# One 64-column product in place of two 32-column products in a hybrid attention and DeltaNet layer

## The chip, the core and the metric

The kernel runs on one core of a Trainium2 chip. The metric is the device time of one execution in microseconds (us), lower is better. Four compute engines with separate instruction streams share the core's memory: TensorE (PE: matmuls into PSUM, with PEld for its weight loads), VectorE (DVE), ScalarE (ACT) and GpSimd (POOL). SyncE (SP) issues the transfers. PSUM has eight banks of 128 partitions by 512 fp32 values here, and the kernel hands them out itself.

## What is computed

One layer over 512 latent tokens and 256 context tokens, width 1024: a modulated RMS norm, one input projection, two mixers side by side (windowed attention, and a gated DeltaNet in both directions), a gated merge, an output projection and an MLP of width 4096. The change lies in the DeltaNet, in its chunked form with chunks of 64 tokens and 8 heads of 64:

```python
def gated_delta_chunked(q, k, v, g_log, beta, s0):
    ...
    kk = jnp.einsum('bhnid,bhnjd->bhnij', kc, kc)
    t_mat = jnp.eye(CHUNK, dtype=jnp.float32) + bc[..., :, None] * dec_strict * kk
    ...
    w_mat = lax.linalg.triangular_solve(t_mat, (bc * eG)[..., None] * kc, ...)
    u_v = lax.linalg.triangular_solve(t_mat, bc[..., None] * vc, ...)
    intra = dec_incl * jnp.einsum('bhnid,bhnjd->bhnij', qc, kc)
    ...
```

`kk` (keys against keys) and `intra` (queries against keys) are 64 by 64 matrices, one for each chunk and head: 4 context and 8 latent chunks, 8 heads.

## The kernel before

**Half products.** `half_products` (L743 to L755) makes the 64 by 64 matrix of 16 pairs of chunk and head pair at a time (a group: four chunks, four head pairs `q`; the two heads of a pair are the two halves `a` of the partitions). Each matrix is cut into four 32 by 32 blocks. For a half `h` of the chunk's keys as weights (64 partitions by 32 columns), x = 0 multiplies with the same half of the chunk (a block on the diagonal, into bank `D_`), x = 1 with the other half (a block off the diagonal, into bank `O_`). So a pair has 8 calls of `PE.matmul` at L754 (two x, two `h`, two `a`), a group 128. All are fp32, and the hardware makes two weight loads and two matmuls of each call. Output partitions are `quad(a, h)`: the four combinations of `a` and `h` use four different tiles of the array. After 8 of the 16 pairs the generator yields, and its caller lets other work in.

**Where it is called.** `chunk_mats(gi)` (L757 to L798) runs for `gi` = 0 (context), 1 and 2 (latent) with keys on both sides. It takes the banks `kD` and `kO`, makes the products, then for each of two directions multiplies masks with the decay (L768, L772), sums the decays by two matmuls each into `dp` and `dO` (L773, L774), takes Exp on ACT (`act`, whose line is L148), and multiplies by beta and mask (L784) and by `kD` (L786). Last it does the same for the off-diagonal part (L793, L794 with `kO`), and frees the banks. This runs woven with the attention's input projections (`in_tile_steps`, matmuls at L313 to L315 of `mm3`; QK norm with L439 on PE, L442 to L450 on DVE, L436 and L437 on ACT). The matrices then go to `invert_all`: a forward substitution on DVE (L827, L828), woven in the same manner.

The second call stands in the main body (L1225 to L1236, called IA stage here): for g = 0 and 1 the queries are multiplied with the keys of group 1 + g, into banks `qD` and `qO`; DVE multiplies by the decay (L1233 for each direction, L1234) and ACT spreads the result (L1241 to L1243). Between the halves PE gets matmuls of the gate tiles as fill (`run_fill`, L998). Behind it come the steps of the scan (`chain_step`, L1110 to L1159), whose first lines do not need these results.

**What sets the order.** Program order and the weaving are written by hand; a scheduler at build time then moves independent instructions of an engine against each other as operands and banks come free. Each engine runs its stream in order. `bank(n)` takes n neighbouring free banks in rotation; in the IA stage four of the eight are held by `zb` (L1093). Input-projection weights go through a cast on ACT (L259) and a subtraction on DVE (L262) before PE can use them (L315 needs L262's result).

Of the kernel before, what the change touches and what calls it, by code (L numbers as in the profile page):

```python
# [12 lines left out]
ALU = mybir.AluOpType  # L13
# [31 lines left out]
CH = 64  # L45
HC = CH // 2
# [53 lines left out]
def tile_layer(ctx: ExitStack, tc: tile.TileContext, I: dict, out: bass.AP, dbg=None):  # L100
    nc = tc.nc
    V, A, G, PE = nc.vector, nc.scalar, nc.gpsimd, nc.tensor
# [19 lines left out]
    alloc, bank = mem.get, lambda n=1: banks.get(n * 512)  # L122
# [17 lines left out]
    def act(out_, in_, func, **kw):  # L140

        sets = TABLES.get(func)
        if sets and actg["set"] not in sets:
            head = A.preload_act_table_set(sets[0])
            for o in actg["ops"]:
                tc.add_manual_dep(head.ins, o.name, nosync, reason="table sets")
            actg.update(set=sets[0], head=head.ins, ops=[head.ins])
        r = A.activation(out_, in_, func, **kw)  # L148
        if sets:
            tc.add_manual_dep(r.ins, actg["head"].name, nosync, reason="table sets")  # L150
            actg["ops"].append(r.ins)
        return r
# [183 lines left out]
    for kt in range(KT):  # L336
        t = alloc(512)
        o = kt * 1024
        hx.append(modulate(t.ap, xt[kt], rx, modA[:, kt, 0:1], modS[:, kt, 0:1],
                           H[:, o:o + 512], H[:, o + 512:o + 1024]))  # L340
        h = alloc(512)
# [313 lines left out]
    kT = [alloc(TOK, True) for _ in range(4)]  # L655
# [37 lines left out]
    def col(c):  # L693

        return SEQ + c * CH if c < NCC else (c - NCC) * CH
# [3 lines left out]
    quad = lambda a, h: slice(64 * a + 32 * h, 64 * a + 32 * h + 32)  # L699
# [38 lines left out]
    ED = [alloc(1024, True) for _ in range(2)]  # L738
    EO = alloc(1024, True)
    NTO = [alloc(512, True) for _ in range(3)]  # L740
    v3 = lambda ap, n=HC: ap.rearrange("p (m i) -> p m i", i=n)

    def half_products(D_, O_, gi, src):  # L743

        for i in range(16):
            if i == 8:
                yield
            c, q = gi * 4 + i // 4, i % 4
            for x, dst in enumerate((D_, O_)):
                for h in range(2):  # L750
                    for a in range(2):
                        r = slice(64 * a, 64 * a + 64)
                        o, o2 = col(c) + HC * h, col(c) + HC * (h ^ x)
                        PE.matmul(dst[quad(a, h), i * HC:(i + 1) * HC], kT[q][r, o:o + HC], src[q][r, o2:o2 + HC],  # L754
                                  start=True, stop=True)  # L755

    def chunk_mats(gi):  # L757
        ms = slice(gi * 16, gi * 16 + 16)
        kD, kO = bank(), bank()
        for _ in half_products(kD, kO, gi, kT):  # L760
            for _ in range(HPAUSE):
                yield
        yield
        dO = bank()
        for d in range(2):
            mg, mb = alloc(1024), alloc(512)
            row = lambda m_: m_[:, d, :].unsqueeze(1).broadcast_to([P, 16, HC])
            V.tensor_tensor(v3(mb.ap), row(nmask), bc(btok[:, d, ms], HC), op=ALU.mult)  # L768
            dp = bank()
            for x in range(2):  # L770
                gx = mg[:, x * 512:x * 512 + 512]
                V.tensor_tensor(v3(r32(gx)), row(mi), bc(gsp[:, x, d, ms], HC), op=ALU.mult)  # L772
                PE.matmul(dp.ap, trr[:, d, :], r32(gx), start=(x == 0), stop=(x == 1))  # L773
                PE.matmul(dO.ap, trr[:, 2 + d, :], r32(gx), start=(d == x == 0), stop=(d == x == 1))  # L774
            mg.free()
            if gi == 0:
                eb = alloc(512)
                e, na = eb.ap, neg[0][:, d * 512:d * 512 + 512]
            else:
                o = (gi - 1) * 512  # L780
                e, na = ED[d][:, o:o + 512], neg[1 + d][:, o:o + 512]
            act(e, dp.ap, AF.Exp)
            dp.free()
            V.tensor_tensor(e, e, mb.ap, op=ALU.mult)  # L784
            mb.free()
            V.tensor_tensor(na, e, kD.ap, op=ALU.mult)  # L786
            if gi == 0:
                eb.free()
            yield
        eb = alloc(512) if gi == 0 else None  # L790
        e = eb.ap if gi == 0 else EO[:, (gi - 1) * 512:gi * 512]
        act(e, dO.ap, AF.Exp)
        V.tensor_tensor(v3(e), v3(e), bc(tbO[:, ms], HC), op=ALU.mult)  # L793
        V.tensor_tensor(NTO[gi].ap, e, kO.ap, op=ALU.mult)  # L794
        for b in (kD, kO, dO, eb):
            if b:
                b.free()
        yield  # L798
# [92 lines left out]
    qT = []  # L891
# [8 lines left out]
    def mats():  # L900
        for q in range(4):
            l2n(kT[q].ap, 1.0, ((0, SEQ), (SEQ, TOK)), epsc, False)
            yield
        for gi in range(3):
            yield from chunk_mats(gi)
# [179 lines left out]
    def run_fill(n):  # L1085
        for _ in range(n):
            next(fill, None)
# [126 lines left out]
    for g in range(2):  # L1214
        ms = slice(16 * g, 16 * g + 16)
        f, b = xa[0][:, ms], xa[1][:, ms]
# [7 lines left out]
    ia = [v64(b.ap) for b in IA]  # L1224
    for g in range(2):  # L1225
        ms = slice(16 * g, 16 * g + 16)
        es = slice(512 * g, 512 * g + 512)
        run_fill(FILL[2] - FPAUSE)
        qD, qO = bank(), bank()
        for _ in half_products(qD, qO, 1 + g, qT):  # L1230
            run_fill(FPAUSE)
        for d in range(2):
            V.tensor_tensor(ia[d][:, ms, :HC], v3(ED[d][:, es]), v3(qD.ap), op=ALU.mult)  # L1233
        V.tensor_tensor(EO[:, es], EO[:, es], qO.ap, op=ALU.mult)  # L1234
        qD.free()
        qO.free()  # L1236
        eo = v3(EO[:, es])
        for a in range(2):
            lo, hi = quad(a, 0), quad(a, 1)
            for d in range(2):  # L1240
                A.activation(ia[d][hi, ms, HC:], ia[d][hi, ms, :HC], AF.Copy)  # L1241
            A.activation(ia[0][lo, ms, HC:], eo[lo], AF.Copy)
            A.activation(ia[1][hi, ms, :HC], eo[hi], AF.Copy)  # L1243
            G.memset(ia[0][hi, ms, :HC], 0.0)
            G.memset(ia[1][lo, ms, HC:], 0.0)
# [52 lines left out]
    for ct in range(8):  # L1298
# [3 lines left out]
        g = gdt[ct].ap  # L1302
# [41 lines left out]
    ms = [(r32(HM[:, k * 1024:k * 1024 + 512]), r32(HM[:, k * 1024 + 512:k * 1024 + 1024])) for k in range(KT)]  # L1344
# [51 lines left out]
    for hf in range(4):  # L1396
        act_ = []
        for f in range(FT):
            if first:
                bufs, _, acc = first.pop(0)  # L1400
# [5 lines left out]
            r, hl = alloc(1024), alloc(1024)  # L1406
# [135 lines left out]
```

## Time and profile before

| | |
|---|---|
| median of 3 runs | 935.47 us (935.13 to 935.96) |
| the profiled execution's own time | 939.21 us |
| its span, first to last instruction | 937.3 us |
| mean granted TensorE clock | 0.991 |
| PE, PEld, DVE, ACT busy, share of the span | 96%, 78%, 64%, 48% |
| PE matmuls, and as many weight loads | 7722 |
| of these at L754 | 1280 |

Terms of the profile: a row "a <- b: us" says that a sat idle until b ended. "Issue" is idle time in which an engine waited for nothing that the profile shows. Rows in order of time have the start, the length and the number of instructions of a run, and in brackets the idle time before it. A matmul's length runs from its start to its modelled end, so the pace of a run of n matmuls is (length of the run minus length of one) / (n - 1).

### The profile page before, as it was taken

How to read it: one execution, taken by the hardware profiler on the slowest of the kernel's cores; microseconds unless marked ns; L12 is line 12 of the kernel's file. 1: busy time of each engine (PE TensorE's matmuls, PEld its weight loads, DVE VectorE, ACT ScalarE, POOL GpSimd, SP SyncE). 2: the span in 40 equal slices, each digit the busy share in tenths (PEclk: the TensorE clock that was granted, in tenths of full speed). 3: DMA queues.
4: the chain of work that ended last, by engine and by line, in shares of the span. 5: the costliest groups of instructions: out<-in, count | busy, mean ns of one | idle time of the engine just before them, and what ended most of it. 6: DMA issues, size and time to landing. Idle time of an engine off the chain costs nothing.

```text
span 937.3 us, 18134 instructions
## 1 busy us (share of the span) xinstructions
PE 902.6 (96%) x7722; PEld 727.8 (78%) x7722; DVE 598.7 (64%) x1021; ACT 448.3 (48%) x827; POOL 12.1 (1%) x26
## 2 busy tenths in 40 slices
PE   8999889989999999989999998999999999999998
PEld 5668667867777677778878888988888888888886
DVE  3588789997887898257865977982455235434411
ACT  5577544347567887475555434560243125213400
POOL 0000000000000002000000000000000000000000
PEclk9999989999999999999999999999999999999999
DMA  9650112110000132225424574481344124222111
GB/s 360 236 198 1 48 47 68 46 45 24 23 13 23 52 108 82 90 93 175 152 83 135 160 267 135 143 288 41 114 146 144 45 68 154 93 68 90 45 43 47
DMA packets 28448, 98.32 MB, mean 105 GB/s; under 512 B 3536, under 2 KB 4176, under 8 KB 27344
## 3 DMA queue, kind: packets, MB, share of 16 engines
q1 hardware_dynamic: 28368, 97.18, 31.7%
q8 instruction: 60, 0.98, 0.4%
q14 instruction: 20, 0.16, 0.1%
HBM read 95.07 MB, written 2.10 MB: 104 GB/s over the span
## 4 chain that ended last, share of the span: by engine, by line
PE 76%; DVE 10%; ACT 6%; DMA 4%; issue 3%; SPq 0%; DVEq 0%; ACTq 0%
PE banks L313 16%; PE banks L314 15%; PE banks L315 15%; PE banks L998 10%; PE banks L1043 2%; PE banks L1110 2%; DMA wr<-in_wm 2%; PE banks L571 1%; DVE wl L262 1%; PE banks L1141 1%; DMA wa<-in_wada 1%; PE banks L1122 1%; DVE m L185 1%; PE banks L577 1%; DVE m L828 1%
## 5 line engine op out<-in xcount | busy, mean ns | idle before, releaser
L313 PE MATMUL banks<-m,m 128*128 128x512 f32 (+1 forms) x600 | 223.6, 378 | 2.7 <-DVE m L620 1.9
L314 PE MATMUL banks<-m,m 128*128 128x512 f32 (+1 forms) x600 | 224.6, 376 | 0.1
L315 PE MATMUL banks<-m,m 128*128 128x512 f32 (+1 forms) x600 | 224.5, 376 | 0.0
L259 ACT ACTIVATE m<-wr 128x1024 fp32r<-128x1024 f32 x68 | 72.1, 1060 | 158.7 <-PE banks L314 79.9
L313 PEld LDWEIGHTS banks<-m,m 128*128 128x128 f32 x600 | 111.9, 188 | 25.5 <-ACT m L319 2.5
L314 PEld LDWEIGHTS banks<-m,m 128*128 128x128 f32 x600 | 112.5, 188 | 22.5 <-issue 1.1
L315 PEld LDWEIGHTS banks<-m,m 128*128 128x128 f32 x600 | 112.5, 188 | 21.6 <-issue 1.2
L262 DVE TENSOR_TENSOR m<-wr,m 128x1024 fp32r<-128x1024 f32 x68 | 83.1, 1224 | 71.2 <-ACT m L259 35.0
L313 PE MATMUL banks<-m,wh 128*128 128x512 f32 (+1 forms) x280 | 104.0, 372 | 0.8 <-ACT wh L259 0.8
L998 PE MATMUL banks<-m,wh 128*128 128x512 f32 x320 | 104.0, 400 | 0.0
L315 PE MATMUL banks<-m,wl 128*128 128x512 f32 (+1 forms) x280 | 101.9, 366 | 1.8 <-DVE wl L262 1.8
L314 PE MATMUL banks<-m,wh 128*128 128x512 f32 (+1 forms) x280 | 101.1, 361 | 0.0
L1426 DVE SCALAR_TENSOR_TENSOR m<-banks,modT,m 128x512 f32<-128x512 f32 x32 | 24.0, 750 | 101.0 <-PE banks L315 101.0
L262 DVE TENSOR_TENSOR wl<-wr,wh 128x1024 fp32r<-128x1024 f32 (+1 forms) x58 | 62.2, 1072 | 28.8 <-ACT wh L259 28.7
L259 ACT ACTIVATE wh<-wr 128x1024 fp32r<-128x1024 f32 (+1 forms) x58 | 54.6, 941 | 30.6 <-PE banks L314 16.8
L998 PEld LDWEIGHTS banks<-m,wh 128*128 128x128 f32 x320 | 59.1, 188 | 12.1
L998 PE MATMUL banks<-m,wl 128*128 128x512 f32 x160 | 64.9, 406 | 0.0
L315 PEld LDWEIGHTS banks<-m,wl 128*128 128x128 f32 x280 | 53.6, 193 | 10.2 <-DVE wl L262 2.6
L313 PEld LDWEIGHTS banks<-m,wh 128*128 128x128 f32 x280 | 54.1, 193 | 9.2 <-ACT wh L259 1.4
L314 PEld LDWEIGHTS banks<-m,wh 128*128 128x128 f32 x280 | 54.1, 193 | 6.9 <-issue 0.2
L184 ACT ACTIVATE m<-m 128x512 fp32r<-128x512 f32 (+1 forms) x56 | 35.2, 631 | 49.2 <-DVE m L1409 21.2
L185 DVE TENSOR_TENSOR m<-m,m 128x512 fp32r<-128x512 f32 (+1 forms) x56 | 38.3, 688 | 18.8 <-ACT m L184 18.3
(236 smaller groups left out, 1298.9 us busy)
## 6 DMA issues: line engine op xcount, KB each, us to landing
wr<-in_wm SPq DMA_DIRECT2D x64, 512.0 KB, 3.5
wr<-in_win SPq DMA_DIRECT2D x38, 512.0 KB, 3.5
wa<-in_wada SPq DMA_DIRECT2D x32, 512.0 KB, 4.3
m<-in_wada SPq DMA_DIRECT2D x8, 1024.0 KB, 11.4
m<-in_xT SPq DMA_DIRECT2D x8, 512.0 KB, 5.3
wr<-in_wbr SPq DMA_DIRECT2D x16, 256.0 KB, 2.6
wr<-in_wout SPq DMA_DIRECT2D x8, 512.0 KB, 4.3
out<-m SPq DMA_DIRECT2D x8, 256.0 KB, 2.0
```

The source lines that it names most:

```text
L184: A.activation(r32(hi), src, AF.Copy)
L185: (eng or V).tensor_tensor(r32(lo), src, hi, op=ALU.subtract)
L259: h = A.activation(r32(hi), raw, AF.Copy)
L262: V.tensor_tensor(r32(lo), raw, hi, op=ALU.subtract)
L313: PE.matmul(acc, w[0][:, k, :], xhi, start=(start and i == 0), stop=False)
L314: PE.matmul(acc, w[0][:, k, :], xlo, start=False, stop=False)
L315: PE.matmul(acc, w[1][:, k, :], xhi, start=False, stop=(stop and i == n - 1))
L571: PE.transpose(pt[:, j * P:(j + 1) * P], probs[j][:, i * P:(i + 1) * P], ident)
L998: PE.matmul(acc.ap, w[x][:, k, :], hx[k][y], start=(k == p == 0), stop=(k == KT - 1 and p == 2))
L1043: PE.matmul(pa.ap, w[x][:, j, :], r32(Q[y][:, :, j, :]), start=(j == p == 0), stop=(j == 3 and p == 2))
L1110: PE.matmul(z[r, x * 256 + q * HD:x * 256 + (q + 1) * HD], src[q][r, col(c):col(c) + CH], S[r, q * HD:(q + 1) * HD], start=True, stop=True)
L1426: V.scalar_tensor_tensor(xn_[ct], acc.ap, modT[:, 3, ct:ct + 1], xn_[ct], op0=ALU.mult, op1=ALU.add)
```

## The change

The two products with x = 0 and x = 1, which have the same weights, become one: the right-hand side is the whole chunk of 64 columns, with its halves in order for `h` = 0 and swapped for `h` = 1, so that the diagonal block comes first in both. A pair of chunk and head pair then takes 4 calls with 64 columns, a group 64 calls, and its output is 64 columns wide, diagonal and off-diagonal block side by side. Eight pairs fill a bank and the group two neighbouring banks, taken by one `bank(2)`. Every reader takes its half as a view: 16 runs of 32 columns, 64 columns apart, over both banks.

```diff
-    def half_products(D_, O_, gi, src):
+    def half_products(dst, gi, src):
...
             c, q = gi * 4 + i // 4, i % 4
-            for x, dst in enumerate((D_, O_)):
-                for h in range(2):
-                    for a in range(2):
-                        r = slice(64 * a, 64 * a + 64)
-                        o, o2 = col(c) + HC * h, col(c) + HC * (h ^ x)
-                        PE.matmul(dst[quad(a, h), i * HC:(i + 1) * HC], kT[q][r, o:o + HC], src[q][r, o2:o2 + HC],
-                                  start=True, stop=True)
+            for h in range(2):
+                for a in range(2):
+                    r = slice(64 * a, 64 * a + 64)
+                    o = col(c) + HC * h
+                    both = src[q][r, col(c):col(c) + CH].rearrange("p (x j) -> p x j", x=2)
+                    PE.matmul(dst[quad(a, h), i * CH:(i + 1) * CH].rearrange("p (x j) -> p x j", x=2),
+                              kT[q][r, o:o + HC], both[:, ::-1] if h else both, start=True, stop=True)
+
+    def diag_off(dst):
+
+        v = dst.ap.rearrange("p (m x i) -> p x m i", x=2, i=HC)
+        return v[:, 0], v[:, 1]
...
-        kD, kO = bank(), bank()
-        for _ in half_products(kD, kO, gi, kT):
+        kk = bank(2)
+        kD, kO = diag_off(kk)
+        for _ in half_products(kk, gi, kT):
...
-            V.tensor_tensor(na, e, kD.ap, op=ALU.mult)
+            V.tensor_tensor(v3(na), v3(e), kD, op=ALU.mult)
...
-        V.tensor_tensor(NTO[gi].ap, e, kO.ap, op=ALU.mult)
-        for b in (kD, kO, dO, eb):
+        V.tensor_tensor(v3(NTO[gi].ap), v3(e), kO, op=ALU.mult)
+        for b in (kk, dO, eb):
...
-        qD, qO = bank(), bank()
-        for _ in half_products(qD, qO, 1 + g, qT):
+        qq_ = bank(2)
+        qD, qO = diag_off(qq_)
+        for _ in half_products(qq_, 1 + g, qT):
             run_fill(FPAUSE)
         for d in range(2):
-            V.tensor_tensor(ia[d][:, ms, :HC], v3(ED[d][:, es]), v3(qD.ap), op=ALU.mult)
-        V.tensor_tensor(EO[:, es], EO[:, es], qO.ap, op=ALU.mult)
-        qD.free()
-        qO.free()
+            V.tensor_tensor(ia[d][:, ms, :HC], v3(ED[d][:, es]), qD, op=ALU.mult)
+        V.tensor_tensor(v3(EO[:, es]), v3(EO[:, es]), qO, op=ALU.mult)
+        qq_.free()
```

The scheduler then places the products and their neighbours anew. In the changed program the products' matmul is still at L754; lines behind it are six higher (L773 is L779, L774 is L780, L998 is L1004, L1110 is L1116).

Two places of PE's stream show it. The first is the second group (`gi` = 1) among the input projections; `m_555` to `m_558` are the keys `kT`, `wh` and `wl` weights of the projection. Before:

```order
L313 MATMUL banks<-m_167,wh_946 128x512
L314 MATMUL banks<-m_167,wh_946 128x512
L754 MATMUL banks<-m_555 32x32 x4
L754 MATMUL banks<-m_556 32x32 x4
...
L439 MATMUL banks<-m_1132,c_bones 128x512
L315 MATMUL banks<-m_167,wl_947 128x512
L754 MATMUL banks<-m_555 32x32 x8
...
L754 MATMUL banks<-m_558 32x32 x8
L313 MATMUL banks<-m_167,wh_946 128x512
```

The same place in the changed program:

```order
L313 MATMUL banks<-m_167,wh_914 128x512
L439 MATMUL banks<-m_1036,c_bones 128x512
L314 MATMUL banks<-m_167,wh_914 128x512
...
L754 MATMUL banks<-m_555 32x64 x4
L754 MATMUL banks<-m_556 32x64 x4
...
L754 MATMUL banks<-m_558 32x64 x4
L315 MATMUL banks<-m_167,wl_915 128x512
L779 MATMUL banks<-m_1117,m_543 128x512 x2
```

Before, the first diagonal products (32 calls) stand 17 projection matmuls behind the last L774 of group 0, then L439, one projection matmul and the other 96 calls. Now all 64 calls stand together, 26 projection matmuls and L439 behind that place, and the first decay matmuls (L779) follow after one projection matmul in place of three.

The second place is the IA stage, second group. `m_1868` to `m_2573` (before: `m_2060` to `m_2765`) are the queries `qT`, L1116 is the first product of a scan step, and the gates are L1004. Before, between the second half of group 0 and the first half of group 1:

```order
L754 MATMUL banks<-m_2765,m_558 32x32 x8
L998 MATMUL banks<-m_167,wl_3971 128x512
...
L998 MATMUL banks<-m_167,wh_4081 128x512 x2
L754 MATMUL banks<-m_2060,m_555 32x32 x8
...
L754 MATMUL banks<-m_2765,m_558 32x32 x8
L998 MATMUL banks<-m_167,wl_4082 128x512
...
L754 MATMUL banks<-m_2765,m_558 32x32 x8
L1110 MATMUL banks<-m_3014,m_555 64x64 x2
```

In the changed program:

```order
L754 MATMUL banks<-m_2573,m_558 32x64 x4
L1004 MATMUL banks<-m_167,wl_3779 128x512
L1004 MATMUL banks<-m_167,wh_3778 128x512 x2
L1004 MATMUL banks<-m_167,wl_3779 128x512
L1116 MATMUL banks<-m_2822,m_555 64x64 x2
...
L1116 MATMUL banks<-m_2824,m_556 64x64
L754 MATMUL banks<-m_1868,m_555 32x64 x4
...
L754 MATMUL banks<-m_2573,m_558 32x64 x4
L1116 MATMUL banks<-m_2824,m_556 64x64
```

Before, 24 gate matmuls lie between the two groups and 12 between the halves of the second. Now 4 gate matmuls and 19 calls of the scan step lie between the groups, the second group's 64 calls stand together, and 13 more calls of the scan step follow them. Both groups use the same two banks (2 and 3) in the changed program; before they used 5 and 2, then 4 and 5.

## The prediction, made before the run

> **What bounds the kernel now.** The page first: PE is busy nearly everywhere, so time comes mostly off PE, unless another engine holds PE up at that place. The last row counts what feeds PE with instructions: 60 packets, 0.98 MB, so 16.4 KB each; with 7722 matmuls and as many weight loads that is 15444 / 60 = 257 instructions a packet.
>
> ```profile
> span 937.3 us, 18134 instructions
> ...
> PE 902.6 (96%) x7722; PEld 727.8 (78%) x7722; DVE 598.7 (64%) x1021; ACT 448.3 (48%) x827; POOL 12.1 (1%) x26
> ...
> q8 instruction: 60, 0.98, 0.4%
> ```
>
> Next PE's waits, whose longest row is the products' own line:
>
> ```profile
> PE banks L754 <- issue: 6.5, 3, 3.2
> ```
>
> PE in order of time shows where. A half group (128 matmul records) runs at (1.29 - 0.19) / 127 = 8.6 ns each. In the second group 64 + 161 records, with their weight loads 450 instructions, start within 4 us, and then PE stands for 3.19 us with nothing to wait for. The third group does the same: 2.52 us. PE waits for its next packet of instructions: from the run at 110.48 to the next record at 115.52 are 5.0 us.
>
> ```profile
> L754 PE MATMUL banks<-m x768: 192/193/214, 91.9 to 132.2; 64*32 64x32 f32 x192
> ...
> 93.55 0.89 PE L754 MATMUL banks<-m 64*32 64x32 f32 x80
> ...
> 97.98 1.29 PE L754 MATMUL banks<-m 64*32 64x32 f32 x128
> ...
> 99.54 0.39 PE L314 MATMUL banks<-m,wh 128*128 128x512 f32 x1
> 99.77 0.40 PE L315 MATMUL banks<-m,wl 128*128 128x512 f32 x1
> ...
> 108.50 0.76 PE L754 MATMUL banks<-m 64*32 64x32 f32 x64 [1.16 <-DVE m L786]
> 109.19 1.12 PE L439 MATMUL banks<-m,c_bones 128*128 128x512 f32 x2
> ...
> 110.48 1.85 PE L754 MATMUL banks<-m 64*32 64x32 f32 x161
> 115.52 0.45 PE L754 MATMUL banks<-m 64*32 64x32 f32 x31 [3.19 <-issue]
> ...
> 128.33 0.72 PE L754 MATMUL banks<-m 64*32 64x32 f32 x60
> 131.57 0.79 PE L754 MATMUL banks<-m 64*32 64x32 f32 x68 [2.52 <-issue]
> ```
>
> The stretches show what follows each stand, in the column behind POOL: a granted clock of 0.57 and of 0.66. They also show DVE: 51.82 of 53.5 us busy from 136.5 on, 23.71 of 25 up to 215. There DVE holds PE up as much as PE holds DVE.
>
> ```profile
> 115.50:119.50 4.00, 3.98 (x40) 3.23 (x41) 0.73 (x2) 0.21 (x1) 0.00 (x0) 0.57 0.02 4
> ...
> 131.50:136.50 5.00, 4.93 (x79) 4.00 (x80) 3.35 (x6) 1.53 (x3) 0.00 (x0) 0.66 0.01 3
> 136.50:190.00 53.50, 53.03 (x285) 43.91 (x284) 51.82 (x112) 21.37 (x35) 0.00 (x0) 1.00 0.17 52
> 190.00:215.00 25.00, 21.97 (x268) 16.02 (x266) 23.71 (x38) 13.71 (x28) 1.04 (x2) 0.93 0.18 59
> ```
>
> Last, DVE in order of time. It stands exactly behind PE's two stands: its L784 needs an Exp of sums that PE makes only after the products.
>
> ```profile
> 110.11 0.68 DVE L794 TENSOR_TENSOR m<-m,banks 128x512 f32<-128x512 f32 x1
> ...
> 119.92 0.69 DVE L784 TENSOR_TENSOR m<-m,m 128x512 f32<-128x512 f32 x1 [3.70 <-ACT m L148]
> ...
> 124.49 0.68 DVE L794 TENSOR_TENSOR m<-m,banks 128x512 f32<-128x512 f32 x1
> ...
> 135.37 0.69 DVE L784 TENSOR_TENSOR m<-m,m 128x512 f32<-128x512 f32 x1 [1.58 <-ACT m L148]
> ```
>
> **Part 1, fewer instructions (removes).** Five groups lose half of their 256 matmul records and as many loads: 1280 instructions, 5 packets. A whole group is now 256 instructions, about one packet, where 450 went into each stand. The densest 5 us in the new order of the chunk stage hold one group (some 2.2 us, part 2) and 2.8 us of projection matmuls at 0.23 us (99.54 to 99.77): 256 + 24 = 280 instructions. Before, 80 + 128 records of L754, some 450 instructions with what lies between, passed from 93.55 to 99.20 without a stand. So I expect both stands to go. PE gets back 3.19 + 2.52, and at the clock 4.0 x 0.43 + 5.0 x 0.34 = 3.4: together 9.1 us.
>
> Not all of it reaches the end. DVE is the next to be late: it gets back 3.70 + 1.58 = 5.28 us, and from there to 215 it has hardly an idle moment, so PE will wait for DVE (for weights split at L262) with the other 3.8. Its work stays the same, and SP's and POOL's streams do not change, so no transfer moves. I carry 5.3 us.
>
> **Part 2, the products themselves.** What does a product with 64 columns cost, on four tiles? No row has it. The nearest have 64 columns of weights on two tiles: with 64 columns on the right (L1110), (1.84 - 0.22) / 53 = 30.6 ns a record, 61 a tile; with 16 on the right (L704), 1.51 / 48 = 31 ns.
>
> ```profile
> L1110 PE MATMUL banks<-m,m x608: 217/218/267, 322.4 to 481.4; 64*64 64x64 f32 x152
> ...
> 407.62 1.84 PE L1110 MATMUL banks<-m,m 64*64 64x64 f32 x54
> 77.75 1.51 PE banks L704 x48
> ```
>
> The lower bound is 8.6 ns (32 more columns free), the upper one 30.6 (only two tiles at a time). I take 61 ns on each of four tiles, 15.3 ns, since four tiles do run beside each other now (8.6 ns is 34 a tile, less than the 61). A half group then takes 64 x 15.3 = 0.98 us against 128 x 8.6 = 1.10: 0.12 less (bounds 0.55 less and 0.86 more). Of ten halves six lie where DVE is the later one; four count: 0.5 us (bounds -2.2 and +3.4).
>
> [...]
>
> **Part 3, the IA stage.** PE loses 0.79 + 0.66 us there to instructions and 0.71 to a bank:
>
> ```profile
> 389.06 1.48 PE L754 MATMUL banks<-m,m 64*32 64x32 f32 x128
> ...
> 393.42 0.97 PE L754 MATMUL banks<-m,m 64*32 64x32 f32 x90
> 395.18 0.53 PE L754 MATMUL banks<-m,m 64*32 64x32 f32 x38 [0.79 <-issue]
> ...
> 402.26 1.27 PE L754 MATMUL banks<-m,m 64*32 64x32 f32 x124 [0.71 <-ACT m L148]
> ...
> 410.13 0.56 PE L1110 MATMUL banks<-m,m 64*64 64x64 f32 x10 [0.66 <-issue]
> ```
>
> The new order packs more small work together: from the second half of the first group on, 128 + 8 + 76 + 256 + 52 + 28 = 548 instructions in about 7 us (1.3 + 0.9 + 1.2 + 2.2 + 0.8 + 0.4, and the starts). Two packets in 7 us, where one took 5, leaves a stand of 0 to 3 us; I take 0.6. New is a wait: the second group uses the first one's pair of banks, so its products stand behind DVE's three reads, and behind them on PE the rest of the scan step and the gates. The reads take 1.28 + 0.68:
>
> ```profile
> 395.68 1.28 DVE L1233 TENSOR_TENSOR m<-m,banks 128x512 f32<-128x512 f32 x2 [5.18 <-PE banks L754]
> 396.89 0.68 DVE L1234 TENSOR_TENSOR m<-m,banks 128x512 f32<-128x512 f32 x1
> ```
>
> DVE was idle for 5.18 us before them, so they start at once and end 1.9 us after the products; the 4 gates and 38 records of L1110 in between take 0.9 + 1.2. Cost 0 to 1; I take 0.5. So 2.16 becomes 1.1: 1.0 us gained (bounds -1.8 and +2.2).
>
> **Part 4, reads through two banks.** 15 reads on DVE step over every other 32 columns. A read of 64 out of 128 columns (L1284) takes 0.741 us, a plain one (L786) 0.679; they are different operations, so 0.06 each is an upper bound: 0.5 us for the nine in the DVE-bound stretch. I take nothing, as the columns of a run lie together in both.
>
> ```profile
> L1284 DVE SCALAR_TENSOR_TENSOR m<-banks,gdnh,m x4: 740/741/751, 499.0 to 502.8; 128x512 f32<-128x512 f32 x4
> L786 DVE TENSOR_TENSOR m<-m,banks x6: 678/679/689, 107.2 to 140.6; 128x512 f32<-128x512 f32 x6
> ```
>
> **Part 5, an added wait in the chunk stage.** Both banks of a group now hold diagonal and off-diagonal blocks, so no product of the next group can start before L794 has read; before, diagonal products needed only L786. Queued behind a waiting product are L315 of the projection and the decay sums that L784 needs. The new order has nine more projection matmuls and L439 ahead of the products, 2.1 + 1.1 us, which bring PE from 107.3 (108.50 less its wait of 1.16) to 110.5; L794 ends at 110.8 now. Cost on PE 0.3 to 1 us a group, covered by the 3.8 us that PE has to spare there.
>
> **The sum.** 5.3 + 0.5 + 1.0 = 6.8 us off the profiled execution: 939.21 to 932.4. That execution lay 3.74 us above the median of 935.47; I take the same difference off the median: 928.7.
>
> **The rivals.** They use one more row, the Exp of 128 by 512:
>
> ```profile
> 401.61 0.60 ACT L148 ACTIVATE m<-banks 128x512 f32<-128x512 f32 x1
> ```
>
> All of PE's time counts. If DVE does not hold PE up, because L262 and the reads move forward too, 9.1 + 1.2 + 1.0 = 11.3 us: 924.2. For it: PE is busy for 53.03 of 53.5 us. Against it: DVE's 51.82. 0.10.
>
> Columns are free. [...] 5.3 + 2.2 + 1.0 = 8.5: 927.0. For it: 16 and 64 columns cost the same at L704 and L1110. Against it: this leaves open what 64 columns need by themselves, up to 61 ns a tile. 0.10.
>
> The chain takes the place of the stands. From one L794 to the next lie products 2.2 us, twelve matmuls up to the last sum 2.7, Exp 0.6, and on DVE L784 to L794 with L442, seven operations, 4.2: 9.7, and some 10.5 with the hand-overs. DVE's own work between L794 at 110.11 and the next, 14.4 us on less 3.7 idle, is 10.7. These are so close that ACT being late by 3 us a group would eat the 5.3, and only 1.5 stays: 934.0. 0.18.
>
> Slower: the tiles take turns. If two right-hand halves in two pieces made products run one at a time, at 61 ns, a half group would take 3.9 us, 2.8 more. Six in the chunk stage: 16.9 - 3.8 to spare - 5.3 = 7.8 more; four in the IA stage: 11.2 - 1.0 = 10.2 more; 953.5. It decides against the change from 36 ns a record on: 0.64 x (36 - 17.2) is the 10.1 of those gains and 1.9 more. Against it: now 8.6 ns with different right-hand sides on all four tiles, into one bank. 0.07. [...]
>
> **How the numbers follow.** My forecast keeps 0.55, with its bounds 926 to 932. About 0.2% (1.9 us) can be told from no change: faster is below 933.6, slower above 937.3. Faster: 0.55 + 0.10 + 0.10 and a little of the chain, 0.04. Same: most of the chain, 0.13. Slower: the tiles and the chain's tail, 0.08. The range leaves out only the tiles and tails: it goes from the first rival, 924, to the chain with the upper bound of part 4 and the lower bound of part 3, 936.
>
> **What would show it.** In the profile after: 640 records at L754, 55 instruction packets; no issue wait at L754 in the chunk stage and a clock of 1.00 behind each group; L784's two waits gone; L754 at about 15 ns a record; in the IA stage at most a stand of 1 us at the second group. Stands that stay or move refute part 1; PE idle for the whole 9 us before 215 would show that DVE gave nothing; a pace above 30 ns refutes part 2.

## The result, and the profile after

The changed kernel takes 930.47 us (median of 8 executions, 928.71 to 934.37); 8 executions of the kernel before beside it had a median of 935.72. The ratio is 0.9948, with a 95% interval of 0.9926 to 0.9971. The time lies inside the forecast range, 1.8 us above the forecast. Run once more in a later group of experiments, the changed kernel gave 931.61 us beside 934.03, ratio 0.9964 (0.9947 to 0.9981): a gain is clear, its size only to within some 2 us.

The profiled execution took 929.72 us, its span 927.7. The page has 640 matmuls and five instruction packets fewer:

```profile
span 927.7 us, 16848 instructions
...
PE 894.8 (96%) x7082; PEld 721.1 (78%) x7082; DVE 597.7 (64%) x1021; ACT 447.6 (48%) x827; POOL 12.1 (1%) x26
...
q8 instruction: 55, 0.90, 0.4%
```

PE in order of time, chunk stage. The second and third group are one row each now, 128 records on end, and neither has a stand in it; a record takes (1.99 - 0.22) / 127 = 13.9 ns. The last row is a new wait, for a weight split on DVE.

```profile
96.56 1.10 PE L754 MATMUL banks<-m 64*32 64x64 f32 x64
...
109.76 1.99 PE L754 MATMUL banks<-m 64*32 64x64 f32 x128
...
120.51 1.99 PE L754 MATMUL banks<-m 64*32 64x64 f32 x128
...
125.23 0.50 PE L779 MATMUL banks<-m,m 128*128 128x512 f32 x1 [0.68 <-DVE m L778]
...
138.24 0.50 PE L530 MATMUL banks<-m,m 128*128 128x512 f32 x1 [0.54 <-ACT m L148]
...
142.15 1.01 PE L315 MATMUL banks<-m,wl 128*128 128x512 f32 x2 [3.10 <-DVE wl L262]
```

That the stands of before were waits for instructions is what the prediction read from counts of instructions. The transfers of the trace show it. In the 3.19 us up to 115.52 before, one packet of instructions (16 KB) was fetched, from 113.18 to 114.14, and PE went on 1.4 us after it had landed:

```profile
q8 instruction: 1, 0.02, 1.9%
```

In the 2.52 us up to 131.57 it was the same: landed at 130.23, PE on at 131.57. In the profiles of all 14 kernel runs named in this document PE sat idle 30 times for over 0.6 us with nothing to wait for, and each time it went on 1.2 to 1.5 us after a packet had landed (1.28 to 1.47 us in the six cases of the profiles before and after). A packet has no fixed 5 us, though: two of them started 3.46 us apart before and 3.41 us apart after.

DVE in the same stretch: L790 (L784 before) waits for nothing any more, DVE is busy nearly without a break (the stretches below), and two reads from the pair of banks take 1.28 us as before. DVE comes to the split that PE wants (L262) only at 140.88, behind a transpose and a sum for the inversion (L813, L929) that stand ahead of it in its queue.

```profile
116.11 1.29 DVE L790 TENSOR_TENSOR m<-m,m 128x512 f32<-128x512 f32 x2
117.32 1.28 DVE L792 TENSOR_TENSOR m<-m,banks 128x512 f32<-128x512 f32 x2
...
127.24 0.69 DVE L790 TENSOR_TENSOR m<-m,m 128x512 f32<-128x512 f32 x1
...
136.47 2.10 DVE L813 STREAM_TRANSPOSE m<-m 128x1024 f32<-128x1024 f32 x1
138.46 0.65 DVE L445 TENSOR_TENSOR m<-m,m 128x512 f32<-128x512 f32 x1
139.03 1.22 DVE L929 TENSOR_TENSOR m<-m,m 128x1024 f32<-128x1024 f32 x1
...
140.88 1.22 DVE L262 TENSOR_TENSOR wl<-wr,wh 128x1024 fp32r<-128x1024 f32 x1
```

The stretches show the clock (behind POOL). It stays at 1.00 behind the products, but drops at the wait for the split: 5.00 x 0.41 + 5.00 x 0.28 = 3.45 us of clock lost, so 6.9 us at half.

```profile
120.00:125.00 5.00, 4.55 (x139) 3.40 (x137) 5.00 (x8) 0.98 (x2) 0.00 (x0) 1.00 0.28 96
...
130.00:135.00 5.00, 4.85 (x23) 3.84 (x21) 5.00 (x8) 2.72 (x5) 0.00 (x0) 1.00 0.00 0
135.00:140.00 5.00, 3.09 (x11) 1.82 (x11) 5.00 (x6) 2.87 (x5) 0.00 (x0) 1.00 0.01 3
140.00:145.00 5.00, 2.85 (x9) 2.46 (x10) 4.91 (x11) 1.26 (x2) 0.00 (x0) 0.59 0.35 91
145.00:150.00 5.00, 5.00 (x22) 4.24 (x21) 4.91 (x13) 1.26 (x2) 0.00 (x0) 0.72 0.19 32
...
160.00:190.00 30.00, 30.00 (x172) 25.41 (x171) 29.04 (x62) 9.55 (x16) 0.00 (x0) 1.00 0.18 54
190.00:215.00 25.00, 22.60 (x360) 16.53 (x359) 20.77 (x40) 17.99 (x37) 2.07 (x4) 1.00 0.15 43
```

The IA stage has neither the two stands nor the wait for the pair of banks. PE waits for ScalarE instead, at the gate matmuls (L1004):

```profile
381.74 1.10 PE L754 MATMUL banks<-m,m 64*32 64x64 f32 x64 [0.19 <-ACT m L148]
...
389.19 1.99 PE L754 MATMUL banks<-m,m 64*32 64x64 f32 x128
...
394.41 0.73 PE L1004 MATMUL banks<-m,wh 128*128 128x512 f32 x2 [1.92 <-ACT m L148]
401.99 1.22 PE L1004 MATMUL banks<-m,wh 128*128 128x512 f32 x4 [1.12 <-ACT wh L259]
```

To see where the time went I cut PE's records at fixed places, the n-th record of a line, the same in every kernel: the 77th and the 164th L313 (92.5 and 176.4 us before) hold the chunk stage, from there to the 168th L848 (377.2; in `combine`, which joins the blocks of the inverse) is the middle, and up to the 299th L1110 (440.0) the IA stage. "Idle" is time with no matmul running, "products" the time from each product's start to the next record's start without idle. "At full clock" takes off half of PE's running time at half clock, since one kernel's time at half clock differs from one execution to the next: the granted clock of the kernel before was 0.992 to 0.998 over the 23 executions of one group.

| | before | after | difference |
|---|---|---|---|
| chunk stage: length | 83.94 | 80.42 | -3.52 |
| of it PE idle | 7.44 | 6.20 | -1.24 |
| of it products | 7.72 | 5.56 | -2.16 |
| at full clock | 80.5 | 77.6 | -2.9 |
| middle: length | 200.76 | 198.17 | -2.59 |
| of it PE idle | 9.14 | 7.55 | -1.59 |
| at full clock | 199.1 | 198.2 | -0.9 |
| IA stage: length | 62.80 | 60.60 | -2.20 |
| of it PE idle | 4.58 | 4.30 | -0.28 |
| of it products | 5.51 | 3.98 | -1.53 |
| rest, to the end | 497.3 | 497.3 | 0 |

At full clock that is 2.9 + 0.9 + 2.2 = 6.0 us; the medians of the two groups of runs lie 5.3 and 2.4 us apart. The profiled pair lies further apart (9.5 us) because the execution of before lost another 1.7 us to a clock drop in the middle, about 1.3 us ahead of the chunk stage, and 0.6 us more than after to the clock in that stage.

### The profile page after: what moved, and what is told of

The parts are those of the page before. It is cut to its first block, busy times and chain, and to the rows that moved or that the text cites. A ratio compares the mean times of both kernels' runs of the same rounds, so it can differ in the third digit from the quotient of the medians.

```text
span 927.7 us, 16848 instructions
## 1 busy us (share of the span) xinstructions
PE 894.8 (96%) x7082; PEld 721.1 (78%) x7082; DVE 597.7 (64%) x1021; ACT 447.6 (48%) x827; POOL 12.1 (1%) x26
## 4 chain that ended last, share of the span: by engine, by line
PE 77%; DVE 11%; ACT 6%; DMA 3%; issue 2%; SPq 0%; DVEq 0%; ACTq 0%
PE banks L313 17%; PE banks L315 16%; PE banks L314 16%; PE banks L1004 10%; PE banks L1049 2%; PE banks L1116 2%; DVE wl L262 2%; PE banks L571 1%; PE banks L1147 1%; DMA wa<-in_wada 1%; PE banks L1128 1%; PE banks L577 1%; PE banks L639 1%; DVE m L834 1%; DVE m L833 1%
## 5 line engine op out<-in xcount | busy, mean ns | idle before, releaser
L313 PE MATMUL banks<-m,m 128*128 128x512 f32 (+1 forms) x600 | 223.3, 377 | 2.7 <-DVE m L620 1.9
L259 ACT ACTIVATE m<-wr 128x1024 fp32r<-128x1024 f32 x68 | 71.9, 1058 | 159.0 <-PE banks L314 80.4
L313 PEld LDWEIGHTS banks<-m,m 128*128 128x128 f32 x600 | 111.8, 188 | 25.8 <-ACT m L319 2.5
L262 DVE TENSOR_TENSOR m<-wr,m 128x1024 fp32r<-128x1024 f32 x68 | 83.1, 1224 | 71.7 <-ACT m L259 35.4
L1004 PE MATMUL banks<-m,wh 128*128 128x512 f32 x320 | 103.6, 400 | 3.0 <-ACT m L148 1.9
L313 PE MATMUL banks<-m,wh 128*128 128x512 f32 (+1 forms) x280 | 104.0, 372 | 1.8 <-DVE m L595 1.0
L262 DVE TENSOR_TENSOR wl<-wr,wh 128x1024 fp32r<-128x1024 f32 (+1 forms) x58 | 62.1, 1071 | 28.6 <-ACT wh L259 28.5
L1004 PEld LDWEIGHTS banks<-m,wh 128*128 128x128 f32 x320 | 58.9, 188 | 15.6 <-ACT m L148 2.2
L1004 PE MATMUL banks<-m,wl 128*128 128x512 f32 x160 | 64.7, 404 | 0.0
L313 PEld LDWEIGHTS banks<-m,wh 128*128 128x128 f32 x280 | 54.4, 194 | 10.2 <-DVE m L595 1.3
```

The lines of the kernel that those rows point to most:

```text
L259: h = A.activation(r32(hi), raw, AF.Copy)
L262: V.tensor_tensor(r32(lo), raw, hi, op=ALU.subtract)
L313: PE.matmul(acc, w[0][:, k, :], xhi, start=(start and i == 0), stop=False)
L1004: PE.matmul(acc.ap, w[x][:, k, :], hx[k][y], start=(k == p == 0), stop=(k == KT - 1 and p == 2))
```

## Experiments

My theory (A) was that the halved count of instructions makes the gain, because PE no longer stands for packets; with it (F) went that DVE, not PE, then sets the chunk stage. The rivals: the products' own pace (D), the pair of banks and the new order (C, E), that PE still sets the stage (G), or a chunk stage in which nothing is to be gained (B). Ratios are to the kernel before in the same group of runs; each is of 6 to 12 executions.

**One stage alone.** First the chunk stage alone, with the IA stage as before:

```diff
-        qq_ = bank(2)
-        qD, qO = diag_off(qq_)
-        for _ in half_products(qq_, 1 + g, qT):
+        qD, qO = bank(), bank()
+        for _ in half_old(qD, qO, 1 + g, qT):
...
```

> The 64-column products in the chunk stage alone; the IA stage as before (two banks, 32-column products). Theory A (fewer instructions a group, so PE no longer stands for its next packet; the stages add up): 57 packets, no issue wait of PE at the products of the chunk stage, the issue waits of 0.8 and 0.7 us in the IA stage are back; the two chunk-stage groups pass as in the changed kernel, some 4 us earlier than before by 180 us, and about 2 us of the change's gain are missing: 932 to 933.5. Rival B (the gain lies in the IA stage and what follows, and the chunk stage is held by DVE anyway): no better than 935.

Measured: 932.04 us, ratio 0.9969 (0.9956 to 0.9981), 57 packets, no stand at the products of the chunk stage; at full clock this stage has 77.7 us, like the changed kernel's (77.6). The IA stage has its stands again, of 1.07 and 1.17 us. B falls.

Then the IA stage alone, with `chunk_mats` as before and the old function for its products:

```diff
-        kk = bank(2)
-        kD, kO = diag_off(kk)
-        for _ in half_products(kk, gi, kT):
+        kD, kO = bank(), bank()
+        for _ in half_old(kD, kO, gi, kT):
...
```

> The 64-column products in the IA stage alone; the chunk stage as before. Theory A: 58 packets, the stands of about 3.2 and 2.5 us at the second and third group of the chunk stage are there as before, no stand in the IA stage, 1 to 2 us faster than before: 933.5 to 934.7. Rival B: nearly all of the gain, 930 to 932.

Measured: 934.03 us, ratio 0.9995 (0.9978 to 1.0011), 58 packets, and the stands of before (3.14 and 2.24 us). The time is as expected, but the interval holds no change too. By the ratios the two parts give 0.31 and 0.05%, together 0.36%, where the two runs of the whole change gave 0.52 and 0.36%. The stages add up within the intervals, which are as wide as the smaller part.

**Same layout and order, as many instructions as before.**

```diff
-            for h in range(2):
-                for a in range(2):
-                    both = src[q][r, col(c):col(c) + CH].rearrange("p (x j) -> p x j", x=2)
-                    PE.matmul(dst[quad(a, h), i * CH:(i + 1) * CH].rearrange("p (x j) -> p x j", x=2),
-                              kT[q][r, o:o + HC], both[:, ::-1] if h else both, start=True, stop=True)
+            for x in range(2):
+                for h in range(2):
+                    for a in range(2):
+                        o, o2 = col(c) + HC * h, col(c) + HC * (h ^ x)
+                        w = i * CH + x * HC
+                        PE.matmul(dst[quad(a, h), w:w + HC], kT[q][r, o:o + HC], src[q][r, o2:o2 + HC],
+                                  start=True, stop=True)
```

> The changed kernel (pair of banks, blocks side by side, both groups of readers stepping over 32 columns), but each product of 64 columns made as two of 32: as many instructions as before, in a still denser row (512 of them on end in the second and third group). Theory A (the count of instructions decides): 60 packets; PE stands for 2.5 to 4 us at each of these two groups, with a half clock behind them, and the time is that of before or a little more: 935 to 938. Rival C (the pair of banks and the new order of the work decide, not the count): 930 to 932, PE without those stands.

Measured: 936.54 us, ratio 1.0019 (0.9997 to 1.0041), 60 packets. PE in order of time has the stands, the longest in the second group of the IA stage; the one in the third group of the chunk stage, 1.92 us, is shorter than the 2.5 I expected, and no half clock follows it:

```profile
111.08 2.06 PE L755 MATMUL banks<-m 64*32 64x32 f32 x220 [0.27 <-DVE m L801]
116.07 0.59 PE L755 MATMUL banks<-m 64*32 64x32 f32 x36 [2.94 <-issue]
...
130.21 0.81 PE L755 MATMUL banks<-m 64*32 64x32 f32 x70 [1.92 <-issue]
...
396.59 1.28 PE L755 MATMUL banks<-m,m 64*32 64x32 f32 x128 [0.49 <-issue]
401.69 1.29 PE L755 MATMUL banks<-m,m 64*32 64x32 f32 x79 [3.82 <-issue]
```

In all, the layout and the order alone bring nothing; C falls for the whole. Against the changed kernel, at full clock, the chunk stage is 1.5 us longer (79.1 for 77.6) and the IA stage 3.7 us (64.3 for 60.6). But C holds for a part: in the chunk stage PE reaches the weight split at 145.97, which before it reached at 148.85, and counted from the same record ahead of the stage (92.7 and 92.5) that is 3.1 us earlier, with stands of 2.94 and 1.92 us still there. DVE's waits for the Exps fell by as much, from 5.5 to 2.5 us (DVE's waits between 100 and 190 us, before and here):

```profile
DVE m L784 <- ACT m L148: 5.5, 3, 3.7
```
```profile
DVE m L791 <- ACT m L148: 2.5, 3, 1.9
```

By this one profile a stand of PE costs there what DVE waits behind it, not its length.

**As many instructions, twice the columns.**

```diff
-                    PE.matmul(dst[quad(a, h), i * CH:(i + 1) * CH].rearrange("p (x j) -> p x j", x=2),
+                    for _ in range(2):
+                        PE.matmul(dst[quad(a, h), i * CH:(i + 1) * CH].rearrange("p (x j) -> p x j", x=2),
...
```

> The changed kernel with every 64-column product issued twice into the same place (the second overwrites the first with the same values): instructions as before, columns doubled. Theory A: 60 packets; stands of 1.5 to 3.5 us at the second and third group, and each half group 64 records x 13.9 ns = 0.9 us longer; the records' pace stays at 14 ns, 936 to 941. Rival D (the 64-column product's own pace is what the change gains by, instructions cost nothing): no stands, only the 0.9 us a half where PE is the later one: 932 to 934.

Measured: 939.00 us, ratio 1.0045 (1.0028 to 1.0062), 60 packets. PE in order of time:

```profile
112.26 3.37 PE L755 MATMUL banks<-m 64*32 64x64 f32 x221 [0.89 <-DVE m L801]
116.90 0.80 PE L755 MATMUL banks<-m 64*32 64x64 f32 x35 [1.26 <-issue]
...
131.15 1.30 PE L755 MATMUL banks<-m 64*32 64x64 f32 x68 [1.21 <-issue]
```

The stands come back (1.2 to 1.8 us; I had said 1.5 to 3.5), and the pace stays at (3.37 - 0.22) / 220 = 14.3 ns. Set beside the run before: 256 records last from 111.08 to 116.66 there, 5.6 us, and from 112.26 to 117.70 here, 5.4 us, although one record takes 9 and 14 ns. The packet sets the end (it landed at 114.68 there and at 115.54 here, 1.4 us ahead of the last records each time); the slower pace only fills the wait. D falls.

**The kernel before, its products handed out in smaller pieces.**

```diff
-            if i == 8:
+            if i and i % step == 0:
                 yield
...
-        for _ in half_products(kD, kO, gi, kT):
+        for _ in half_products(kD, kO, gi, kT, 2):
...
```

Each piece is followed by one pause in place of two.

> The kernel before, with its 32-column products and two separate banks, the chunk stage's products only handed out in eight pieces of 32 calls' eighth (7 pauses a group in place of 2 behind the first half); the IA stage as before. As many instructions as before, but the third group's calls lie in pieces of 8 to 32 between projection matmuls; the second group still has 24 + 72 calls close together. Theory A (PE stands where more than a packet falls into a packet's 5 us, whatever the products look like): 60 packets, a stand of 2 to 3 us at the second group, none over 0.5 us at the third; DVE's wait of 1.6 us behind the third goes: 933 to 935. Rival E (the count over the stage matters, or the new order and the pair of banks alone): both stands as before, 935 to 937.

Measured: 935.86 us, ratio 1.0012 (0.9998 to 1.0027). The stands are as theory A has them, 2.34 us in the second group and none in the third, but the gain is missing: A's time was wrong here, and it is E's. DVE's wait for its Exps fell from 5.5 to 1.8 us:

```profile
DVE m L784 <- ACT m L148: 1.8, 3, 0.9
```

Yet the chunk stage of the profile is only 1.8 us shorter (82.14 for 83.94), although no half clock falls into it, and 1.6 us longer at full clock: cut into more runs the products take 8.38 us for 672 records, where 720 took 7.72, and the sums for the norms (L439) between them 5.21 for 3.88. At least 2 us of what the stand no longer takes, PE spends on the same work in smaller pieces.

**Mask products on GpSimd.**

```diff
-            V.tensor_tensor(v3(mb.ap), row(nmask), bc(btok[:, d, ms], HC), op=ALU.mult)
+            G.tensor_tensor(v3(mb.ap), row(nmask), bc(btok[:, d, ms], HC), op=ALU.mult)
```

> The changed kernel with the six products of the mask and the betas (nmask times btok, 128 by 512 each, 0.68 us on DVE) made on GpSimd. Theory F (DVE now sets the chunk stage, PE has time to spare there): DVE has 4.1 us less, PE's waits for DVE in this stage (0.7, 0.6 and 3.1 us) shrink by 2 to 4 us in all, 927 to 929. Rival G (PE sets it): nothing, 930 to 931.5. Rival H: GpSimd's products take over 2 us each or hold DVE up while they run: 930 to 934.

Measured: 931.63 us, ratio 0.9961 (0.9941 to 0.9980): the changed kernel's. The reason fits H, with smaller numbers. GpSimd takes 1.4 to 1.9 us for one in this stage, and a pair of DVE's products that meets one takes 2.1 us for 1.3 (in order of time, the two engines):

```profile
105.62 1.49 POOL L774 TENSOR_TENSOR m<-c_nmask,btok 128x512 f32<-128x512 f32 x1 [15.46 <-PE banks L315]
107.73 1.43 POOL L774 TENSOR_TENSOR m<-c_nmask,btok 128x512 f32<-128x512 f32 x1 [0.62 <-DVE m L790]
```
```profile
106.12 2.14 DVE L790 TENSOR_TENSOR m<-m,m 128x512 f32<-128x512 f32 x2
...
118.84 2.15 DVE L790 TENSOR_TENSOR m<-m,m 128x512 f32<-128x512 f32 x2
```

This run could not tell F from G, so a later one took the work off altogether.

**Smaller pieces in the changed kernel.**

```diff
-HPAUSE = 2
+HPAUSE = 1
```

> The changed kernel with one pause in place of two behind each half of the chunk stage's products: pieces of at most 32 calls with projection matmuls between them. Theory A: a whole group already fits one packet, so spreading it further brings nothing on PE, no stand in either; what remains is DVE's order (a weight split moves by a few operations): 929.5 to 932, the same as the changed kernel. Rival E: the order of the work makes the gain, and this one moves it by 2 us or more either way.

Measured: 930.08 us, ratio 0.9956 (0.9936 to 0.9976): no difference from the changed kernel, as A said. At full clock the chunk stage has 77.8 us.

**No gate matmuls between the halves, IA stage.**

```diff
-FPAUSE, CPAUSE = 12, 12
+FPAUSE, CPAUSE = 0, 12
```

> The changed kernel with no gate matmuls between the two halves of a group's products in the IA stage: all 64 calls on end, then the scan step. Theory A (density decides): 64 calls are 256 instructions in 2 us, and the scan step's small products follow: a stand of 0.5 to 2 us behind the second group, 930.5 to 933. Rival E: no stand, 929.5 to 930.5.

Measured: 929.03 us, ratio 0.9938 (0.9914 to 0.9963). No stand at the products, and the time is a little better than E's. This does not test A, though: the second group does not stand on end as I expected, six gate matmuls come behind its first 42 records. In order of time PE's wait for ScalarE falls from 1.92 + 1.12 to 1.10 us:

```profile
385.87 1.99 PE L754 MATMUL banks<-m,m 64*32 64x64 f32 x128
...
390.58 0.85 PE L754 MATMUL banks<-m,m 64*32 64x64 f32 x42
391.37 0.50 PE L1004 MATMUL banks<-m,wl 128*128 128x512 f32 x1
...
392.96 1.41 PE L754 MATMUL banks<-m,m 64*32 64x64 f32 x82
...
395.47 0.73 PE L1004 MATMUL banks<-m,wh 128*128 128x512 f32 x2 [1.10 <-ACT m L148]
```

The IA stage is 1.8 us shorter than the changed kernel's (58.83 for 60.60; idle 1.98 for 4.30).

**DVE's work in the chunk stage made less.** The betas are left out, so this kernel does not compute the layer; it is there for its time.

```diff
-            V.tensor_tensor(v3(mb.ap), row(nmask), bc(btok[:, d, ms], HC), op=ALU.mult)
...
-            V.tensor_tensor(e, e, mb.ap, op=ALU.mult)
+            V.tensor_tensor(v3(e), v3(e), row(nmask), op=ALU.mult)
```

> The changed kernel with the product of the mask and the betas left out of the chunk stage: the masks are applied directly, the betas not at all (one DVE operation of 128 by 512 fewer for each of six half groups). Theory F (DVE sets the stage up to the weight split that PE waits for): five of these operations lie between 92 and 140 us, 5 x 0.6 = 3.0 us; that split ends about 3 us earlier, PE's wait for it (3.1 us) shrinks only as far as PE's own work allows, and the stage to 175 us is 1.5 to 3 us shorter: 927.5 to 929.5. Rival G (PE sets it): no change, 930 to 931.5.

Measured: 928.02 us, ratio 0.9929 (0.9903 to 0.9955), where the changed kernel in the same group of runs had 931.61 and 0.9964. F holds: with nothing taken off PE, the chunk stage falls from 77.6 to 75.4 us at full clock, and in order of time PE's wait for the split is shorter and ends 2.5 us earlier, counted from the 77th L313 (with the half clock behind it gone as well):

```profile
141.20 0.62 PE L315 MATMUL banks<-m,wl 128*128 128x512 f32 x2 [1.88 <-DVE wl L262]
```

**The weight split ahead of the inversion's transpose** (with no fill in the IA stage, as above; the transposes are handed out after the split, and the split is tied behind the third group's last read).

```diff
+        if len(o800) == 3:
+            tc.add_manual_dep(l.ins, o800.pop().ins.name, nosync, reason="behind the last group")
...
-    run_inv(INV[0])
+    run_inv(0)
```

> The changed kernel with two moves: no gate matmuls between the halves of a group's products in the IA stage (as in the run before without fill), and on DVE the weight split that PE waits for behind the chunk stage placed directly behind the last group's reads, ahead of the second 32 by 32 transpose (2.1 us) and the sum (1.2 us). Theory F: PE's wait of 3.1 us falls below 1 us, and the half clock behind it (3.4 to 6.8 us long) goes with it, 2 to 4 us: 925.5 to 928. Rival I: the wait moves to the next weight split or to the scores, which need what stands behind it on DVE, and the time stays at 929.

Measured: 931.52 us, ratio 0.9973 (0.9958 to 0.9988): the ratio lies above the 0.9938 without this move, though the two intervals just overlap. F's first half came true: PE's wait for the split and the half clock are gone, the chunk stage is 74.3 us long in place of 80.4. The middle gives it back: 204.0 us for 198.2, PE idle 12.6 for 7.55, and 3 us more up to the end. Its waits for DVE in the middle are new or longer (the lines are 4 or 5 higher than in the changed kernel):

```profile
PE banks L317 <- DVE m L599: 2.4, 2, 1.6
PE banks L1009 <- DVE m L592: 1.3, 1, 1.3
PE banks L582 <- DVE m L185: 1.2, 2, 0.8
PE banks L858 <- DVE m L848: 1.0, 1, 1.0
```

I has the mechanism right, but not the time: it said 929. DVE has as much to do as before, and what is moved back in its queue is missed later.

**The changed kernel again.**

> The changed kernel once more, as a measure beside the two others: 929.5 to 931.5 under every theory; the half clock of 3.4 to 6.8 us behind PE's wait for the weight split at about 140 us is there again if that wait causes it.

Measured: 931.61 us, ratio 0.9964 (0.9947 to 0.9981), 0.1 us over what I expected. Every stage length is within 0.3 us of the first profile's, and the half clock stands at the same place behind the same wait (3.08 us).

**One pause and no fill together**: the two edits above at once.

> The changed kernel with one pause in place of two behind each half of the chunk stage's products and no gate matmuls between the halves of a group's products in the IA stage, both at once. In the single runs PE's time from the combine to the fifth scan step was 1.8 us shorter without the fill (58.8 for 60.6), and the chunk stage no longer with one pause. If stages add up: PE's time over these two stages as in the single runs to 0.3 us, and the time 1 to 2 us below the changed kernel, 928 to 930, 0.4 to 0.65% below the kernel before. If the IA stage's gain is given back later, as the earlier weight split's was: 930 to 931.5.

Measured: 930.35 us beside 935.67, ratio 0.9939 (0.9917 to 0.9962). The time is 0.35 us over the range I gave, the ratio inside it. At full clock its chunk stage has 77.8 us, as with one pause alone, and its IA stage 59.9, 1 us more than without fill alone, where I had expected no more than 0.3 of difference. This one and the one without fill have the lowest ratios of all complete kernels, but their intervals overlap with the changed kernel's: the IA stage's profiles suggest that they beat it, the times do not settle it.

The stages account for the times to about 2.4 us. At full clock, the gain over the kernel before up to the end of the span, worked out from one profile each, beside the measured ratio times 935 us:

| kernel | chunk | middle | IA | rest | sum | measured |
|---|---|---|---|---|---|---|
| changed | 2.9 | 0.9 | 2.2 | 0 | 6.0 | 4.9 |
| changed again | 2.9 | 0.6 | 2.4 | -0.1 | 5.8 | 3.4 |
| chunk stage alone | 2.8 | 1.0 | -0.4 | -0.8 | 2.6 | 2.9 |
| IA stage alone | 0.3 | -0.2 | 3.1 | -1.3 | 1.9 | 0.5 |
| 32 columns, new layout | 1.4 | 0 | -1.5 | -0.5 | -0.6 | -1.8 |
| issued twice | -2.3 | 0.3 | -2.3 | 0.5 | -3.8 | -4.2 |
| before, spread | -1.6 | 0.8 | 1.3 | 0.7 | 1.2 | -1.1 |
| masks on GpSimd | 2.7 | 0.1 | 2.2 | -1.5 | 3.5 | 3.6 |
| one pause | 2.7 | 0.6 | 1.8 | -1.6 | 3.5 | 4.1 |
| no fill | 2.9 | 0.7 | 4.0 | -1.1 | 6.5 | 5.8 |
| betas left out | 5.1 | -0.1 | 1.9 | -1.0 | 5.9 | 6.6 |
| split first, no fill | 6.2 | -4.9 | 4.1 | -3.1 | 2.3 | 2.5 |
| one pause, no fill | 2.7 | 0.5 | 2.9 | 0.1 | 6.2 | 5.7 |

Unchanged parts scatter by up to 1.6 us (the rest, but for the kernel with the split first), so differences below that are not read from this table. The largest misses are 2.4 us for the changed kernel's second run and 2.3 for the kernel before with its products spread, where even the sign is wrong.

## Why the prediction was right, and where its terms were off

The total was right: 6.8 us forecast, 6.0 by the stages at full clock, 5.3 and 2.4 by the medians of two groups. The mechanism of part 1 was right up to the weight split. That the sum came so near is partly luck, since part 1 was too large and parts 2 and 3 too small. The range was wide as well: from 924 to 936 it held the kernel before too. Its upper end does not come out of its terms: the chain's 934.0, with 0.5 for part 4 and 2.8 from 1.0 gained to 1.8 lost in part 3, is 937.3.

**Part 1 (carried 5.3).** The stands went, with five packets, and DVE took over: PE's new wait is for a split at L262, the line named. The carrying was right up to that split. Before, PE started on it here:

```profile
148.85 0.62 PE L315 MATMUL banks<-m,wl 128*128 128x512 f32 x2 [0.23 <-DVE wl L262]
```

Now it starts at 142.15, 6.7 us earlier, and 5.4 counted from the 77th L313 (92.5 and 91.2). The step that failed is that "from there to 215" DVE holds PE up, so that PE's 3.8 us to spare cost nothing, with a clock of 1.00 behind the groups. A half clock followed PE's wait of 3.10 us, as it had followed the stands, and behind it PE sets the pace: it is busy for 30.00 of 30 us from 160 to 190, DVE for 29.04. PE ran 5.6 us at half clock there and lost 2.8. With 0.8 us for matmuls of the scores (L530, L531, L542), which PE made ahead of the split and not behind it, 5.4 - 2.8 + 0.8 = 3.4 is what arrived; the stage is 3.5 us shorter. PE's idle time up to the split fell by only 1.2 us, from 7.44 to 6.20: where the two stands had been, there are waits of 1.07, 0.68, 0.57, 0.54 and 3.10 us.

**Part 2 (counted 0.5).** The pace came out well, 13.9 ns for 15.3. Had the added columns cost nothing, it would have been the 8.6 ns of 32 columns, which the trace does not bear out for these products on four tiles. The term was too small all the same: products cost PE 2.16 us less in the chunk stage, where that mostly turned into waiting, and 1.53 in the IA stage, where it counted. Before, the 720 records of the chunk stage took 7.72 us, 10.7 ns each where I had reckoned 8.6 from one undisturbed row, because they were cut into more runs; after, 360 take 5.56 us, 15.4 ns each, nearer to the undisturbed 13.9.

**Part 3 (1.0).** The IA stage gave 2.2 us, but not by the waits I counted. Stands and bank wait went, a stand of 0.6 and the wait for the pair did not come; ScalarE's 1.92 and 1.12 us stood there instead, and idle time fell by only 0.28. The products made 1.53 of the rest. The run with 32-column products shows what the halved count is worth in this order: with it, no stand; without it, 3.82 us at the second group, and the stage 3.7 us longer at full clock.

**Part 4 (0)** held: two reads at L792 take 1.28 us as before at L786, the strided ones at L1240 and L1241 0.68 each. **Part 5** held: PE waits nowhere at the products for L800 in the profile's chunk stage, though one projection matmul does for 0.57 us.

**Not foreseen:** 0.9 us in the middle, less than the table can tell. Two of PE's waits for the scores' chain on DVE are shorter by 1.0 and 0.9 us, while a new one of 1.0 us has come (L313 behind L595). Why is not shown; DVE's work has moved forward (PE's waits between 160 and 285 us, before and after):

```profile
PE banks L530 <- DVE m L620: 1.7, 1, 1.7
PE banks L571 <- DVE m L588: 1.5, 1, 1.5
```
```profile
PE banks L530 <- DVE m L620: 0.7, 1, 0.7
PE banks L571 <- DVE m L588: 0.6, 1, 0.6
```

**The rivals.** All of PE's time counts: refuted by the run without the betas, which gains by DVE alone. Columns are free: refuted by 13.9 ns against 8.6. Tiles take turns: refuted, 36 ns were needed and 13.9 measured. The chain in the stands' place: L790 no longer waits at all in the chunk stage. How the 5.4 us up to the split divide between the count and the new order is known from one profile only: with the old count in the new order 3.1 of them were there.

## What to carry over

A stand of an engine is worth what the next engine in line waits behind it (DVE's 5.3 us for PE's 5.7 here), and only as far down as that engine stays the limit: look at what stands behind the place where the saved time turns into waiting, the clock among it. In the IA stage, where PE's stands gave way to waits for ScalarE, it was the shorter products (1.53 us) that counted. Moving an operation ahead in a full queue brings its waiters forward and sets back those of what it overtakes: the run with the split first gained 3.3 us at full clock in the chunk stage against the one without fill, and paid 7.6 behind it.

## What the runs showed of the hardware

- A packet of instructions set when a dense row of small matmuls ended: 256 records took 5.6 us at 9 ns a record and 5.4 us at 14 ns, with stands of 2.94 and 1.26 us in them. PE went on 1.2 to 1.5 us after a 16 KB packet had landed in all 30 idle times of over 0.6 us without a wait.
- PE's clock dropped behind short waits: in the chunk stage, 11 of 12 waits of 2.2 to 3.2 us were followed by a drop of 3.4 or 6.8 us (one of 2.34 us was not), one of three of 1.9 us, and none that was shorter. Elsewhere a wait of 1.60 us (up to 565.73 before) and one of 1.61 us (up to 556.40 after) were followed by a drop of 3.4 us; one of 1.86 us (up to 68.45 before) and one of 1.92 us (up to 394.41 after) were not.
- Two DVE products from and to SBUF that met a product on GpSimd took 2.14 us for 1.29, 0.85 more; the GpSimd product beside them ran on for 0.99 us after they had started.
